# Decay factors of a gated DeltaNet layer: from matrix products of masked gates to differences of running sums spread by DMA

## The chip, the cores and the metric

The kernel runs on one NeuronCore of one Trainium2 chip. The core has a matrix engine (PE, with its weight loads shown apart as PEld), a vector engine (DVE), a scalar engine (ACT), a general engine (POOL) and a queue processor (SP) that issues most transfers. Each engine takes its instructions in the order in which they stand in its own list, and waits on semaphores of the others. The metric is the device time of one execution in microseconds. Before the change the median of three runs is 1008.61 us (1008.36 to 1009.39).

## The reference

Two layers act on 256 tokens of width 2048. Layer 0 is a gated DeltaNet with 16 heads of 128, layer 1 a banded softmax attention; each is `h = h + Mixer(RMSNorm(h))`. What matters here is how layer 0 gets its decays:

```python
g = -jnp.exp(a_log) * jax.nn.softplus(a_in + dt_bias)      # per token and head
gc = jnp.cumsum(g, axis=-1)
diff = gc[..., :, None] - gc[..., None, :]
decay = jnp.exp(jnp.where(tri_incl, diff, -jnp.inf))       # exp(gc_i - gc_j), lower triangle
lower = jnp.where(tri_strict, (k_beta @ k^T) * decay, 0.0)
qk = (q @ k^T) * decay
```

All weights and activations are float32. The kernel works on two token halves of 128 instead of chunks of 64, so for every head it needs three 128x128 blocks of factors `exp(gc_i - gc_j)`: the first half with itself, the second half against the first, the second half with itself.

## The kernel before, in words

The weights (168 MB) pass through the core once. A weight tile is 512 KB. It arrives in one of four `wt` buffers by a transfer that SP issues (L208), ACT rounds it to the matrix engine's reduced float format (`whi`, the cast at L209), DVE forms what the rounding left (`wlo = wt - whi`, L210), and PE multiplies both with the activations (L259). `whi` and `wlo` have three buffers each, and `LOOK = 3`: in the program's text the cast of tile i+3 stands ahead of the products of tile i, and it can start only when PE has read tile i's `whi` for the last time.

In the part of the program that is changed, the tiles hold 256 columns (the "half" kind). Such a tile takes eight products of 512 columns with `whi` and eight of 256 columns with `wlo`. With even numbers the `whi` products come first, with odd numbers the `wlo` products. Tiles are numbered here in the order of the plan, from 0: tiles 0 to 7 are the first query block, 8 to 15, 16 to 23 and 24 to 31 are the other three query blocks, 32 to 63 the key blocks.

Everything else is side work, written as Python generators in two lanes, `bgq` and `bg2`. After every four products of a half tile the helper `tick` runs a step: it takes turns between the lanes and lets one generator go on to its next `yield`. In the query stage `bgq` holds the short convolutions (`q_conv`, L527 and L529), SiLU and the transposes of the queries (`q_rest`, L546, L552, squares at L558), and `bg2` holds `decays()`, which makes the factors. The built order of each engine is then set by the framework's scheduler, which goes by its own estimate of times and by these positions; it doesn't change at run time.

`decays()` first computes the gates `g` for 128 tokens x 32 (16 heads, two halves). Until the change it goes on as follows, for four groups of four heads:

- DVE masks: `rhs(gi)` multiplies the lower-triangle mask `lt_f` with the gate of each head, once for the rounded gate `g_r` and once for its rest `gl_r` (L486, four 128x512 instructions a group).
- PE sums: six products of 512 columns a group, with the constant matrices `gt_r` and `ones_r` (L501), into three PSUM tiles. The result is already `gc_i - gc_j`.
- ACT exponentials: two 128x512 instructions (L506, L507) and four of 128x128 with a per-partition bias (L509), out of PSUM into `dec`, which lies in the buffer `dl`.
- DVE masks the two diagonal blocks (L516, two 128x512 instructions a group).

`dec` is used much later, in the key stage (L605), where it multiplies the key and query products. The buffer `tt`, which holds `rhs`'s results, is used again there.

Of the kernel before, what the change touches and what calls it, by code (L numbers as in the profile page):

```python
# [7 lines left out]
F32 = mybir.dt.float32  # L8
F32R = mybir.dt.float32r
# [30 lines left out]
def tile_hybrid_trunk(  # L40
# [22 lines left out]
    def ps_small():  # L63
        return pss.tile([P, 512], F32, name="pss", tag="pss")
# [5 lines left out]
    def slot(tag, kb, dt=F32):  # L70

        return big.tile([P, kb * 256], dt, name=tag, tag=tag)
# [12 lines left out]
    for _ in range(NWARM):  # L85
# [11 lines left out]
    gt_f = abm[:, 1024 + P:1024 + 2 * P]  # L97
    pool.memset(gt_f, 1.0)
    pool.affine_select(out=gt_f, in_=gt_f, compare_op=ALU.is_gt, fill=0.0, base=0,
                       pattern=[[-1, P]], channel_multiplier=1)  # L100
# [4 lines left out]
    gt_r = const.tile([P, P], F32R, name="gt_r")  # L105
    ones_r = const.tile([P, P], F32R, name="ones_r")
# [301 lines left out]
    def ht(name, dt=F32):  # L408
        return const.tile([P, H, 2], dt, name=name)

    beta, g_r, gl_r = ht("beta"), ht("g_r", F32R), ht("gl_r", F32R)
# [8 lines left out]
    def decays():  # L420
        act.copy(out=gt_r, in_=gt_f)
        act.copy(out=ones_r, in_=ones_f)

# [51 lines left out]
        dve.tensor_copy(out=g_r, in_=q)  # L475
        dve.tensor_tensor(out=gl_r, in0=q, in1=g_r.bitcast(F32), op=ALU.subtract)
        yield 1
        dve.tensor_scalar(out=eb, in0=eb, scalar1=1.0, scalar2=None, op0=ALU.add)
        dve.reciprocal(out=beta, in_=eb)

        rbuf = slot("tt", 16, F32R).rearrange("p (b k c) -> p b k c", b=2, k=4)

        def rhs(gi):
            for half in range(2):
                for part, src in ((0, g_r), (1, gl_r)):
                    dve.tensor_tensor(  # L486
                        out=rbuf[:, gi % 2, 2 * half + part, :].rearrange("p (h c) -> p h c", h=4),
                        in0=lt_f.unsqueeze(1).broadcast_to([P, 4, P]),
                        in1=src[:, 4 * gi:4 * gi + 4, half].bitcast(F32).unsqueeze(2).broadcast_to([P, 4, P]),
                        op=ALU.mult)  # L490

        rhs(0)
        yield 1
        rhs(1)
        yield 1
        for gi in range(4):
            hs = slice(4 * gi, 4 * gi + 4)
            ps3 = [ps_small() for _ in range(3)]
            for dst, lhs, half in ((ps3[0], gt_r, 0), (ps3[1], ones_r, 1), (ps3[2], gt_r, 1)):
                for part in range(2):  # L500
                    pe.matmul(dst, lhsT=lhs, rhs=rbuf[:, gi % 2, 2 * half + part, :],  # L501
                              start=(part == 0), stop=(part == 1))
            v0 = ps3[0].rearrange("p (h c) -> p h c", h=4)
            tail = tiny.tile([P, 4], F32, name="tail", tag="tail")
            dve.tensor_copy(out=tail, in_=v0[:, :, P - 1])
            act.activation(out=dec[:, hs, 0:128], in_=v0, func=AF.Exp)  # L506
            act.activation(out=dec[:, hs, 256:384], in_=ps3[2].rearrange("p (h c) -> p h c", h=4), func=AF.Exp)  # L507
            for i in range(4):
                act.activation(out=dec[:, 4 * gi + i, 128:256], in_=ps3[1][:, i * P:(i + 1) * P], func=AF.Exp,  # L509
                               bias=tail[:, i:i + 1])  # L510
            yield 1
            if gi < 2:
                rhs(gi + 2)
            yield 1
            for c in (0, 256):
                dve.tensor_tensor(out=dec[:, hs, c:c + 128], in0=dec[:, hs, c:c + 128],  # L516
                                  in1=lt_f.unsqueeze(1).broadcast_to([P, 4, P]), op=ALU.mult)
            yield 1
# [730 lines left out]
```

## Time and profile before

| | |
|---|---|
| median of three runs | 1008.61 us |
| the profiled execution | 1010.83 us, its span 1009.1 us |
| PE busy | 1001.4 us (99%), 6090 matmul records |
| DVE busy | 690.0 us (68%) |
| ACT busy | 526.6 us (52%) |
| POOL busy | 62.4 us (6%) |
| DMA | 177.57 MB, mean 176 GB/s |
| group L486 (masked gates), DVE | 16 instructions, 5.2 + 5.1 us |
| group L501 (sums), PE | 24 instructions, 5.3 + 2.6 us |
| groups L506, L507, L509 (exponentials), ACT | 24 instructions, 2.4 + 2.4 + 4.5 us |
| group L516 (masks), DVE | 8 instructions, 5.3 us |

A row of a group gives line, engine, operation, the tiles that it writes and reads, the shape, the count, then the busy time in us and the mean duration of one in ns, and behind a second bar the idle time of the engine ahead of it and what ended that. A row of the timeline gives start and duration in us, then engine, line, operation and count of one run of equal instructions. Since instructions of an engine overlap a little, the distance from one start to the next is what an instruction costs its engine, and is less than its duration. The first L501 starts at 82.4 us, the last at 103.7 us. The granted clock (PEclk) is the share of TensorE's full clock that the chip allows.

### The profile page before, as it was taken

To read this page: it belongs to the slowest core of one execution; us is meant where nothing else is said; L and a number is where in the kernel's file an instruction comes from. 1 tells how busy PE (TensorE), PEld (TensorE's weight loads), DVE (VectorE), ACT (ScalarE), POOL (GpSimd) and SP (SyncE) were. 2 spreads that over 40 slices of the span, in tenths; PEclk is the share of its full clock that TensorE was granted. 3 is DMA by queue.
4 is the path that set the end of the run, shared out by engine and by line. 5 is a ranking of instruction groups with operands and counts; after the bars stand their busy time and mean duration, and the time that the engine had idled before them with its cause. 6 is when DMAs were issued, how large, how long until landed. Compare 5 with 4: busy or idle time off the path is not lost.

```text
span 1009.1 us, 15660 instructions
## 1 busy us (share of the span) xinstructions
PE 1001.4 (99%) x6090; PEld 878.8 (87%) x6090; DVE 690.0 (68%) x1121; ACT 526.6 (52%) x784; POOL 62.4 (6%) x83
## 2 busy tenths in 40 slices
PE   8999999999999999999999999999999999999998
PEld 7988888888888899899988888888888888889987
DVE  5789979997998767755867555444456666666554
ACT  6557865565446555534645444444445555555432
POOL 1000001022000000001000000000011010101000
PEclk8999999999999999999999999999999999999999
DMA  8665565555665454535765776666665565554472
GB/s 285 169 169 167 158 185 145 160 160 167 197 186 163 131 148 145 167 127 180 237 188 183 224 219 204 193 191 194 199 186 169 148 178 155 167 157 157 158 230 92
DMA packets 134186, 177.57 MB, mean 176 GB/s; under 512 B 7904, under 2 KB 90208, under 8 KB 134112
## 3 DMA queue, kind: packets, MB, share of 16 engines
q1 hardware_dynamic: 132672, 172.12, 57.5%
q0 software_dynamic: 1152, 4.19, 1.2%
q8 instruction: 47, 0.77, 0.3%
q10 hardware_dynamic: 288, 0.26, 0.1%
q14 instruction: 27, 0.22, 0.1%
HBM read 174.46 MB, written 2.10 MB: 175 GB/s over the span
## 4 chain that ended last, share of the span: by engine, by line
PE 98%; DMA 1%; DVE 0%; ACT 0%; issue 0%; SPq 0%
PE psp L259 87%; PE pss L601 2%; PE pss L259 1%; PE pss L1068 1%; DMA wt<-in_a_w_in_dram 1%; PE pss L1087 1%; PE pss L1123 1%; PE pss L833 1%; PE pss L501 1%; PE pss L1113 1%; PE pss L857 0%; PE pss L856 0%; PE pss L840 0%; PE pss L858 0%; PE pss L1086 0%; PE pss L1124 0%
## 5 line engine op out<-in xcount | busy, mean ns | idle before, releaser
L210 DVE TENSOR_TENSOR wlo<-wt,whi 128x1024 fp32r<-128x1024 f32 (+1 forms) x322 | 391.2, 1218 | 244.9 <-ACT whi L209 241.0
L209 ACT CAST whi<-wt 128x1024 fp32r<-128x1024 f32 (+1 forms) x322 | 336.7, 1046 | 381.3 <-PE psp L259 331.8
L259 PE MATMUL psp<-whi,xb 128*128 128x512 f32 x1024 | 318.9, 391 | 0.0
L259 PE MATMUL psp<-xb,whi 128*128 128x512 f32 (+1 forms) x1088 | 261.4, 382 | 2.2 <-ACT whi L209 1.9
L259 PEld LDWEIGHTS psp<-xb,whi 128*128 128x128 f32 x1088 | 197.0, 191 | 36.4 <-ACT whi L209 2.5
L259 PEld LDWEIGHTS psp<-whi,xb 128*128 128x128 f32 x1024 | 191.7, 188 | 39.1
L259 PE MATMUL psp<-wlo,xb 128*128 128x512 f32 x512 | 200.8, 392 | 0.0
L259 PE MATMUL psp<-xb,wlo 128*128 128x256 f32 x1024 | 149.0, 285 | 0.7 <-DVE wlo L210 0.7
L259 PE MATMUL psp<-g,whi 128*128 128x256 f32 (+1 forms) x736 | 149.6, 318 | 0.0
L259 PEld LDWEIGHTS psp<-xb,wlo 128*128 128x128 f32 x1024 | 138.0, 192 | 6.6 <-DVE wlo L210 1.2
L259 PEld LDWEIGHTS psp<-g,whi 128*128 128x128 f32 x736 | 121.7, 191 | 8.4 <-DVE g L900 0.2
L259 PEld LDWEIGHTS psp<-wlo,xb 128*128 128x128 f32 x512 | 96.2, 188 | 19.7
L259 PE MATMUL psp<-g,wlo 128*128 128x256 f32 x480 | 101.9, 284 | 0.3 <-DVE wlo L210 0.3
L259 PEld LDWEIGHTS psp<-g,wlo 128*128 128x128 f32 x480 | 77.8, 191 | 1.7 <-DVE wlo L210 0.5
L529 DVE SCALAR_TENSOR_TENSOR cv<-raw,sm,cv 128x255 f32<-128x255 f32 (+2 forms) x144 | 63.8, 477 | 3.4 <-ACT cv L527 3.2
L527 ACT ACTIVATE cv<-raw,sm 128x256 f32<-128x256 f32 x48 | 22.5, 509 | 20.6 <-DVE raw L345 20.6
L1051 POOL TENSOR_SCALAR ssn<-ssn,uh 128x4 f32<-128x4 f32 x16 | 8.3, 530 | 266.8 <-DVE ssn L1049 266.8
L330 DVE TENSOR_TENSOR ev<-psp,ev 128x512 f32<-128x512 f32 x33 | 22.6, 684 | 0.1
L329 ACT COPY ev<-psp 128x512 f32<-128x512 f32 x33 | 19.1, 579 | 0.0
L1099 ACT ACTIVATE raw<-raw,mx 128x128 f32<-128x128 f32 (+1 forms) x32 | 14.2, 446 | 7.4 <-DVE mx L1097 7.4
L605 DVE TENSOR_TENSOR dl<-pss,dl 128x512 f32<-128x512 f32 (+1 forms) x32 | 16.3, 551 | 2.7 <-PE pss L601 2.7
L1058 DVE TENSOR_TENSOR cv<-psp,rn 128x512 f32<-128x512 f32 x16 | 10.2, 683 | 8.9 <-POOL rn L1053 8.9
(233 smaller groups left out, 742.4 us busy)
## 6 DMA issues: line engine op xcount, KB each, us to landing
wt<-in_b_w_in_dram SPq DMA_DIRECT2D x128, 512.0 KB, 3.7
wt<-in_a_w_in_dram SPq DMA_DIRECT2D x127, 512.0 KB, 4.0
wt<-in_a_w_out_dram SPq DMA_DIRECT2D x32, 512.0 KB, 3.8
wt<-in_b_w_out_dram SPq DMA_DIRECT2D x32, 512.0 KB, 3.9
dl<-in_xT_dram POOLq DMA_DIRECT2D x4, 512.0 KB, 5.8
dl<-in_relb_dram POOLq DMA_DIRECT2D x4, 512.0 KB, 4.9
g<-in_xT_dram SPq DMA_DIRECT2D x7, 256.0 KB, 5.2
out_dram<-cv SPq DMA_DIRECT2D x2, 512.0 KB, 3.5
```

The costliest lines, as they stand in the source:

```text
L209: cast = act.copy(out=hi[:, js, cs], in_=wt[:, js, cs])
L210: rest = dve.tensor_tensor(out=lo[:, js, cs], in0=wt[:, js, cs], in1=hi[:, js, cs].bitcast(F32), op=ALU.subtract)
L259: state["mm"] = pe.matmul(*args, **kw).ins
L329: act.copy(out=ev, in_=ps[:, :, 1, :])
L330: dve.tensor_tensor(out=ev, in0=ps[:, :, 0, :], in1=ev, op=ALU.add)
L501: pe.matmul(dst, lhsT=lhs, rhs=rbuf[:, gi % 2, 2 * half + part, :], start=(part == 0), stop=(part == 1))
L527: act.activation(out=cv[:, i, :], in_=raw[:, i, :], func=AF.Copy, scale=conv_w(i0 + i, 3))
L529: dve.scalar_tensor_tensor(out=cv[:, i, s:], in0=raw[:, i, :T - s], scalar=conv_w(i0 + i, 3 - s), in1=cv[:, i, s:], op0=ALU.mult, op1=ALU.add)
L601: pe.matmul(dst, lhsT=kq[:, a, i, c:c + P], rhs=rhs, start=(n == 0), stop=(n == 2))
L605: dve.tensor_tensor(out=dl[:, h, :, c], in0=src.rearrange("p (k c) -> p k c", k=2), in1=dec[:, h, c].unsqueeze(1).broadcast_to([P, 2, n]), ...
L1058: dve.tensor_tensor(out=n[:, t, :].rearrange("p (h d) -> p h d", d=P), in0=ps[:, t, :].rearrange("p (h d) -> p h d", d=P), in1=rn[:, t, :] ...
L1099: act.activation(out=s[:, a:b], in_=s[:, a:b], func=AF.Exp, bias=mx[:, t:t + 1], accum_out=sums[:, t:t + 1])
```

## The change

The constants `gt_f`, `gt_r` and `ones_r`, the rounded gates and `rhs` go. Two small float32 products with `lt_f` give the running sums of the gates, once with heads on the partitions (32x128) and once with tokens on the partitions (128x32). The first goes by DMA to a DRAM tile `line` and from there, in four transfers of 512 KB, to all 128 partitions of `tt`: every partition then has the running sums of all heads along its row. The second, with its sign changed, is `ngc`. Nine `yield`s follow. Then, for each group of four heads, POOL copies the two diagonal blocks from `tt` to `dec` and writes -1e30 outside the triangle (`affine_select`), and adds the bias `across` for the third block; after a `yield`, ACT takes the exponentials of one head to a `yield`, three 128x128 instructions with a per-partition bias, from SBUF.

```diff
@@ def decays():
-        act.copy(out=gt_r, in_=gt_f)
-        act.copy(out=ones_r, in_=ones_f)
...
-        dve.tensor_copy(out=g_r, in_=q)
-        dve.tensor_tensor(out=gl_r, in0=q, in1=g_r.bitcast(F32), op=ALU.subtract)
-        yield 1
+        gf = q.rearrange("p h t -> p (h t)")
         dve.tensor_scalar(out=eb, in0=eb, scalar1=1.0, scalar2=None, op0=ALU.add)
         dve.reciprocal(out=beta, in_=eb)
...
-        rhs(0)
-        yield 1
-        rhs(1)
-        yield 1
+        yield 1
+        ps = ps_small()
+        pe.matmul(ps[0:32, 0:P], lhsT=gf, rhs=lt_f, start=True, stop=True)
+        pe.matmul(ps[:, P:P + 32], lhsT=lt_f, rhs=gf, start=True, stop=True)
+        grow = abm[0:32, 1280:1280 + P]
+        dve.tensor_copy(out=grow, in_=ps[0:32, 0:P])
+        ngc = const.tile([P, H, 2], F32, name="ngc")
+        dve.tensor_scalar(out=ngc, in0=ps[:, P:P + 32].rearrange("p (h t) -> p h t", t=2), scalar1=-1.0, scalar2=None,
+                          op0=ALU.mult)
+        line = rows.tile([32, P], F32, name="line")
+        nc.gpsimd.dma_start(out=line, in_=grow)
+        gb = slot("tt", 16).rearrange("p (j c) -> p j c", c=P)
+        for gi in range(4):
+            js = slice(8 * gi, 8 * gi + 8)
+            nc.gpsimd.dma_start(out=gb[:, js, :], in_=line[js, :].unsqueeze(0).broadcast_to([P, 8, P]))
+        for _ in range(9):
+            yield 1
+        gb = gb.rearrange("p (h t) c -> p h t c", t=2)
+        across = const.tile([P, H], F32, name="across")
         for gi in range(4):
             hs = slice(4 * gi, 4 * gi + 4)
-            ps3 = [ps_small() for _ in range(3)]
-            for dst, lhs, half in ((ps3[0], gt_r, 0), (ps3[1], ones_r, 1), (ps3[2], gt_r, 1)):
-                for part in range(2):
-                    pe.matmul(dst, lhsT=lhs, rhs=rbuf[:, gi % 2, 2 * half + part, :],
-                              start=(part == 0), stop=(part == 1))
...
-            act.activation(out=dec[:, hs, 0:128], in_=v0, func=AF.Exp)
-            act.activation(out=dec[:, hs, 256:384], in_=ps3[2].rearrange("p (h c) -> p h c", h=4), func=AF.Exp)
-            for i in range(4):
-                act.activation(out=dec[:, 4 * gi + i, 128:256], in_=ps3[1][:, i * P:(i + 1) * P], func=AF.Exp,
-                               bias=tail[:, i:i + 1])
...
-            for c in (0, 256):
-                dve.tensor_tensor(out=dec[:, hs, c:c + 128], in0=dec[:, hs, c:c + 128],
-                                  in1=lt_f.unsqueeze(1).broadcast_to([P, 4, P]), op=ALU.mult)
-            yield 1
+            for t in range(2):
+                pool.affine_select(out=dec[:, hs, 2 * P * t:2 * P * t + P], in_=gb[:, hs, t, :], compare_op=ALU.is_ge,
+                                   fill=NEG, base=0, pattern=[[0, 4], [1, P]], channel_multiplier=-1)
+            pool.tensor_tensor(out=across[:, hs], in0=gb[:, hs, 0, P - 1], in1=ngc[:, hs, 0], op=ALU.add)
+            yield 1
+            for h in range(4 * gi, 4 * gi + 4):
+                for c, src, b in ((0, dec[:, h, 0:P], ngc[:, h, 0:1]), (P, gb[:, h, 1, :], across[:, h:h + 1]),
+                                  (2 * P, dec[:, h, 2 * P:3 * P], ngc[:, h, 1:2])):
+                    act.activation(out=dec[:, h, c:c + P], in_=src, func=AF.Exp, bias=b)
+                yield 1
```

The scheduler moves instructions with it. In the changed kernel the lines behind the removed ones have smaller numbers: L203 is the cast of L209, L204 the rest of L210, L253 the products of L259, L509 the scaling of L527, L528 the SiLU of L546, L534 the transposes of L552, L540 the squares of L558; L499 are the new exponentials.

The first place is ACT, from the first exponentials on. `whi` is the rounded weight tile, `dl` holds `dec`, `sj` is the output of a square that nobody reads, and the tables are the sets of functions that ACT loads. Before, from the last cast ahead of them:

```order
L209 CAST whi<-wt 128x1024 x4
L329 COPY ev<-psp 128x512
L507 ACT_TABLE_LOAD
L507 ACTIVATE dl<-pss 128x4x128
L527 ACTIVATE cv<-raw,sm 128x256 x2
L209 CAST whi<-wt 128x1024
L506 ACTIVATE dl<-pss 128x4x128
L509 ACTIVATE dl<-pss,tail 128x128 x4
L209 CAST whi<-wt 128x1024
L506 ACTIVATE dl<-pss 128x4x128
L509 ACTIVATE dl<-pss,tail 128x128 x4
L209 CAST whi<-wt 128x1024
```

With the change, from the cast of tile 27 over that of tile 28:

```order
L203 CAST whi<-wt 128x1024
L540 ACTIVATE sj,ssq<-pss 128x128 x4
L499 ACT_TABLE_LOAD
L499 ACTIVATE dl<-dl,ngc 128x128 x4
L509 ACTIVATE cv<-raw,sm 128x256 x2
L499 ACTIVATE dl<-dl,ngc 128x128 x3
L499 ACTIVATE dl<-tt,across 128x128 x4
L499 ACTIVATE dl<-dl,ngc 128x128
L203 CAST whi<-wt 128x1024
L499 ACTIVATE dl<-dl,ngc 128x128 x4
L499 ACTIVATE dl<-tt,across 128x128 x2
```

The rows that follow are L499 alone, until the last one of the 48:

```order
L499 ACTIVATE dl<-tt,across 128x128
L499 ACTIVATE dl<-dl,ngc 128x128
L528 ACT_TABLE_LOAD
L528 ACTIVATE g<-cv 128x1024
L203 CAST whi<-wt 128x1024 x3
```

Before, no more than six exponential instructions stood between two casts. Now 12 of the 48 stand between the casts of tiles 27 and 28, and the other 36, a table load and a SiLU between the casts of tiles 28 and 29.

The second place is PE, from the second half of tile 22 on. `pss` are the small PSUM tiles, `psp` the accumulators of the weight products. Before:

```order
L259 MATMUL psp<-xb,wlo 128x256 x14
L501 MATMUL pss<-tt,gt_r 128x512
L259 MATMUL psp<-xb,wlo 128x256 x2
L501 MATMUL pss<-tt,ones_r 128x512
L501 MATMUL pss<-tt,gt_r 128x512
L259 MATMUL psp<-xb,whi 128x512 x2
```

With the change, up to the products of tile 29 (the ten `wlo` products are eight of tile 22 and two of tile 23, the row of eight transposes stands between tiles 28 and 29):

```order
L253 MATMUL psp<-xb,wlo 128x256 x10
L472 MATMUL pss<-kT 32x128
L473 MATMUL pss<-kT 128x32
L534 MATMUL pss<-ident,g 128x128 x12
L253 MATMUL psp<-xb,wlo 128x256 x6
L253 MATMUL psp<-xb,whi 128x512 x16
L534 MATMUL pss<-ident,g 128x128 x4
L253 MATMUL psp<-xb,wlo 128x256 x16
L253 MATMUL psp<-xb,whi 128x512 x16
L253 MATMUL psp<-xb,wlo 128x256 x16
L253 MATMUL psp<-xb,whi 128x512 x16
```

```order
L253 MATMUL psp<-xb,wlo 128x256 x8
L534 MATMUL pss<-ident,g 128x128 x8
L253 MATMUL psp<-xb,wlo 128x256 x8
L253 MATMUL psp<-xb,whi 128x512 x16
```

The 24 sums of L501 are gone, two short products stand in tile 23, and twelve transposes of the queries have moved ahead into tile 23 and four into tile 24.

More of the change, by code (lines that the diff above doesn't have):

```diff
@@ L96, in tile_hybrid_trunk @@
                        pattern=[[1, P]], channel_multiplier=-1)
[L97 to L100, printed above, removed]
     ones_f = const.tile([P, P], F32, name="ones_f")
@@ L104, in tile_hybrid_trunk @@
     pool.memset(nhalf, -0.5)
-    gt_r = const.tile([P, P], F32R, name="gt_r")
-    ones_r = const.tile([P, P], F32R, name="ones_r")
     def rsqrt(dst, src, scale, bias):
@@ L409, in ht @@
         return const.tile([P, H, 2], dt, name=name)
-    beta, g_r, gl_r = ht("beta"), ht("g_r", F32R), ht("gl_r", F32R)
+    beta = ht("beta")
+    rows = ctx.enter_context(tc.tile_pool(name="rows", bufs=1, space=bass.MemoryType.DRAM))
     dl = slot("dl", 48).rearrange("p (h k c) -> p h k c", h=H, k=2)
@@ L474, in decays @@
                                  op0=ALU.mult, op1=ALU.mult)
-        dve.tensor_copy(out=g_r, in_=q)
-        dve.tensor_tensor(out=gl_r, in0=q, in1=g_r.bitcast(F32), op=ALU.subtract)
-        yield 1
+        gf = q.rearrange("p h t -> p (h t)")
         dve.tensor_scalar(out=eb, in0=eb, scalar1=1.0, scalar2=None, op0=ALU.add)
         dve.reciprocal(out=beta, in_=eb)
[L481 to L490, printed above, removed]
@@ L496, in decays @@
         for gi in range(4):
             hs = slice(4 * gi, 4 * gi + 4)
-            ps3 = [ps_small() for _ in range(3)]
-            for dst, lhs, half in ((ps3[0], gt_r, 0), (ps3[1], ones_r, 1), (ps3[2], gt_r, 1)):
-                for part in range(2):
-                    pe.matmul(dst, lhsT=lhs, rhs=rbuf[:, gi % 2, 2 * half + part, :],
-                              start=(part == 0), stop=(part == 1))
-            v0 = ps3[0].rearrange("p (h c) -> p h c", h=4)
-            tail = tiny.tile([P, 4], F32, name="tail", tag="tail")
@@ L505, in decays @@
-            dve.tensor_copy(out=tail, in_=v0[:, :, P - 1])
-            act.activation(out=dec[:, hs, 0:128], in_=v0, func=AF.Exp)
-            act.activation(out=dec[:, hs, 256:384], in_=ps3[2].rearrange("p (h c) -> p h c", h=4), func=AF.Exp)
-            for i in range(4):
-                act.activation(out=dec[:, 4 * gi + i, 128:256], in_=ps3[1][:, i * P:(i + 1) * P], func=AF.Exp,
-                               bias=tail[:, i:i + 1])
-            yield 1
-            if gi < 2:
-                rhs(gi + 2)
```

## The prediction

> **What bounds the kernel now.** I read the page first: busy time, the slices, the chain that ended last.
>
> ```profile
> span 1009.1 us, 15660 instructions
> PE 1001.4 (99%) x6090; PEld 878.8 (87%) x6090; DVE 690.0 (68%) x1121; ACT 526.6 (52%) x784; POOL 62.4 (6%) x83
> PEclk8999999999999999999999999999999999999999
> PE 98%; DMA 1%; DVE 0%; ACT 0%; issue 0%; SPq 0%
> ```
>
> PE is the chain. A busy PE is not yet a PE at its peak, so I looked at the stretch of the change, in windows (PE, PEld, DVE, ACT, POOL, clock, DMA share, GB/s) and in the timeline of PE.
>
> ```profile
> 80.00:90.00 10.00, 10.00 (x61) 8.82 (x60) 10.00 (x16) 5.41 (x8) 0.00 (x0) 1.00 0.55 160
> 90.00:100.00 10.00, 10.00 (x54) 8.58 (x53) 10.00 (x19) 8.82 (x19) 0.00 (x0) 1.00 0.51 138
> 100.00:110.00 10.00, 10.00 (x59) 8.71 (x58) 10.00 (x19) 8.34 (x24) 0.00 (x0) 1.00 0.58 149
> ```
>
> ```profile
> 91.03 3.33 PE L259 MATMUL psp<-xb,whi 128*128 128x512 f32 x14
> 94.20 1.08 PE L501 MATMUL pss<-tt,gt_r 128*128 128x512 f32 x4
> 95.12 1.10 PE L259 MATMUL psp<-xb,wlo 128*128 128x256 f32 x8
> 96.06 1.77 PE L259 MATMUL psp<-xb,whi 128*128 128x512 f32 x7
> ```
>
> From start to start: 14 products in 3.17 us (0.226 each), four sums of L501 in 0.92 (0.23 each), eight `wlo` products in 0.94 (0.118 each). They follow each other without a hole. DVE is full in the same 30 us (10.00 of 10.00), yet PE never waits for it: taking work off DVE wins nothing here, taking work off PE does, one for one. A weight tile costs PE 8 x 0.226 + 8 x 0.118 = **2.75 us**.
>
> How far ahead of PE the tiles are made ready is in the waits of the whole run (total, times, longest).
>
> ```profile
> ACT whi L209 <- PE psp L259: 331.8, 214, 5.1
> DVE wlo L210 <- ACT whi L209: 241.0, 199, 4.3
> ```
>
> ACT's casts wait for PE to free one of three buffers, so the lead is what three buffers hold and no more. Whatever keeps ACT from a cast for longer than that lead stops PE, and PE has no slack anywhere later to win it back.
>
> **The change part by part.**
>
> *PE's work.* 24 sums go: 24 x 0.23 = -5.5 us. Two float32 products come. The nearest row is one that the program has four times and the trace eight, each in two passes:
>
> ```profile
> L387 PE MATMUL pss<-dg,ones_f 128*128 128x128 f32 x8 | 1.2, 274 | 0.0
> ```
>
> 1.2 / 8 = 0.15 a pass, four passes: +0.6. Net **-4.9 us**, all on the path. The moved transposes are the same number as before.
>
> *DVE's work.* Sixteen L486 and eight L516 at some 0.6 us go, two small copies come. Priced at nothing: PE's products covered them, as the windows show. If that cover were gone, wlo rather than these would be late.
>
> *ACT's work, where the stall goes.* 24 exponential instructions become 48, of 128 columns, from SBUF, with a bias per partition. The one row of that very form is in layer 1:
>
> ```profile
> 822.26 1.05 ACT L209 CAST whi<-wt 128x1024 fp32r<-128x1024 f32 x1 [2.98 <-PE psp L259]
> 823.21 0.39 ACT L1099 ACTIVATE raw<-raw,mx 128x128 f32<-128x128 f32 x1
> 823.51 0.19 ACT L1099 ACTIVATION_READ_ACCUMULATOR raw<-raw,mx 128x1 f32 x1
> 100.57 1.13 ACT L509 ACTIVATE dl<-pss,tail 128x128 f32<-128x128 f32 x4
> 111.29 1.28 ACT L546 ACT_TABLE_LOAD   x1
> 112.59 1.06 ACT L546 ACTIVATE g<-cv 128x1024 f32<-128x1024 f32 x1
> 113.55 0.26 ACT L558 ACTIVATE sj<-pss 128x128 f32<-128x128 f32 x1
> 113.71 0.19 ACT L558 ACTIVATION_READ_ACCUMULATOR sj<-pss 128x1 f32 x1
> 113.80 0.27 ACT L558 ACTIVATE sj<-pss 128x128 f32<-128x128 f32 x1
> L210 DVE TENSOR_TENSOR wlo<-wt,whi 128x1024 fp32r<-128x1024 f32 x319 | 389.6, 1224 | 244.3 <-ACT whi L209 240.3 <-PE psp L259 3.3
> L527 ACT ACTIVATE cv<-raw,sm 128x256 f32<-128x256 f32 x48 | 22.5, 509 | 20.6 <-DVE raw L345 20.6
> ```
>
> The exponential of L1099 holds ACT for 823.51 - 823.21 = 0.30 us; L509, out of PSUM, for about 0.25 (four in 1.13, the last one 0.37 long). A whole duration without overlap would be 0.39. I take 0.30, the same operands; ends 0.25 and 0.39. A cast costs ACT 0.95, a SiLU 0.96, a square with its read 0.25, an L527 about 0.4 to 0.5.
>
> The yields ask for three exponentials a step, but ACT follows the built order, where they stand together. I start both clocks at the end of the four transposes in the middle of tile 24, which the squares behind the cast of tile 27 wait for.
>
> ACT from there to the point where tile 29 can start: four squares 1.0, table 1.28, 48 exponentials 14.4, two L527 0.9, cast of tile 28 0.95, table 1.28, SiLU 0.96, cast of tile 29 1.05, and then DVE's rest of tile 29 1.22 (an odd tile begins with `wlo`). Sum **23.0 us**.
>
> PE from there to tile 29: eight `wlo` products 0.9, tiles 25 to 28 4 x 2.75 = 11.0, eight transposes 0.8. Sum **12.7 us**.
>
> So PE stands still for **+10.3 us** ahead of tile 29. Behind the waiting cast are the casts of tiles 30 and 31 and SP's next weight transfer; PE waits for all of them, and they come at 1 us each once ACT is free, faster than PE needs them. The eight transposes wait for the SiLU behind the exponentials and then fit under the cast. The nine yields themselves cost nothing: the factors are first read behind tile 46 of the built order, 17 tiles or 47 us after tile 29.
>
> *The data of the first exponential.* The sums come by two transfers in a row through POOL's queue.
>
> ```profile
> 80.77 1.84 PE L259 MATMUL psp<-xb,wlo 128*128 128x256 f32 x14
> 82.44 0.39 PE L501 MATMUL pss<-tt,gt_r 128*128 128x512 f32 x1
> dl<-in_relb_dram POOLq DMA_DIRECT2D x4, 512.0 KB, 4.9
> dl<-in_xT_dram POOLq DMA_DIRECT2D x4, 512.0 KB, 5.8
> sm<-in_small_dram SPq DMA_DIRECT2D x1, 16.0 KB, 2.2
> L95 POOL TENSOR_SCALAR_AFFINE_SELECT kT<-kT x1: 287/287/287, 1.8 to 1.8; 128x128 f32<-128x128 f32 x1
> L651 POOL MEMSET tt<- 128x4096 f32 x1 | 3.5, 3535 | 17.1 <-PE pss L601 17.1
> ```
>
> On the clock of this trace the eighth of the fourteen `wlo` products ends at about 81.7 and tile 23 begins. DVE copies the sums out behind the rest of tile 25 (1.22, not before 81.7) and one L345: about 83.9. The 16 KB line lands 2.2 to 4.9 us later, the first 512 KB 4.9 to 5.8 after that, a select of 512 columns takes about 0.6 (0.29 for 128, and 3535 / 4096 = 0.86 ns for each further column): data at 91.6 to 95.2. ACT gets there at 81.7 + 0.9 (`wlo`) + 0.6 + 1.3 (twelve transposes) + 16 x 0.226 + 0.4 (four transposes) = 88.5, and 2.3 on for squares and table: 90.8. Late by 0.8 to 4.4; I take **+1.5**, near the lower end, since the line is small. The later three quarters land while ACT works 3.6 us a quarter: 512 KB in 3.6 us is 146 GB/s beside the 138 to 160 of the windows, below the 345 seen here:
>
> ```profile
> 8.00:10.00 2.00, 1.28 (x10) 1.07 (x10) 0.68 (x2) 0.91 (x2) 0.00 (x0) 1.00 0.96 322
> 10.00:12.00 2.00, 0.78 (x2) 0.50 (x2) 1.00 (x2) 1.81 (x3) 0.27 (x1) 0.69 1.06 393
> 12.00:15.00 3.00, 2.54 (x13) 2.52 (x12) 2.55 (x5) 2.55 (x7) 0.49 (x2) 0.50 1.01 345
> 15.00:20.00 5.00, 5.00 (x34) 5.00 (x34) 4.42 (x9) 3.89 (x8) 0.81 (x2) 0.74 1.04 344
> ```
>
> *The clock.* The same rows price what a stall does to PE: after PE had been partly idle from 8 to 12 us, its granted clock was 0.69, 0.50 and 0.74, that is halved for 1.2 + 3.0 + 2.6 = 6.8 us. A stall of 10 us is longer than that one was. Halved for up to 6.8 us of work costs at most 3.4 us; part of it falls into the stall itself. I take **+2.4**, ends 0 and 3.4.
>
> The Trainium skill, page "TensorE: Matmul & The Clock Gate", section "Part 1: The HAM clock gate", has the clock at half after an idle window of about 3.4 us and at full again after one busy window. By that rule the loss would be 1.7 to 3.4 us, and the sum 1017.2 to 1018.9. The 6.8 us here agree with two such windows.
>
> **Sum**, for the profiled execution of 1010.83 us (span 1009.1, 1.7 around it): -4.9 + 10.3 + 1.5 + 2.4 = +9.3, so 1020.1. The median of the runs is 2.2 below that execution: 1008.6 + 9.3 = 1017.9, **1018 us**.
>
> **The rivals.**
>
> *The exponentials hide, faster.* If PE found tile 29 ready, the 24 sums would be won: 1008.6 - 4.9 = **1003.7**. For it speaks that every wait of PE in this stretch is zero today, with up to six exponential instructions between casts. Against it: ACT's 23.0 us would have to fall to 12.7, that is 48 exponentials in 4 us, 0.08 each, where the shortest row of that width is a square out of PSUM at 0.16 (113.55 to 113.71). At that price the stall is 3.6, hardly long enough for the clock, and the data's lateness then makes it about 1008: no change. Both together 11 in 100.
>
> *The spread data starve ACT.* 128 partitions read the same 4 KB, a pattern that no row has, and POOL's selects may be held up:
>
> ```profile
> L625 POOL TENSOR_SCALAR ssk<-ssk x4: 241/778/1161, 173.2 to 247.3; 128x8 f32<-128x8 f32 x4
> L628 POOL TENSOR_TENSOR rk<-rk,beta 128x8 f32<-128x8 f32 x4 | 2.6, 653 | 0.3
> ```
>
> The same operation takes 0.24 or 1.16. With 0.92 more on two selects and one addition a quarter needs 2 x 0.6 + 0.65 + 2.8 = 4.6 us on POOL, 1 us over ACT's 3.6, three times: +3; first data at their late end: +2.9. That is **1024**; with a slow repeated read, more. Against it: DVE, whatever its part, is idle itself while PE stalls. 12 in 100. The Trainium skill ("GPSIMD Engine Reference", "Key points") says that POOL shares its SBUF ports with DVE and is held up by DVE instructions with two SBUF inputs; by that rule the result would be this one, and no row here shows which instruction held L625 up.
>
> *The stall without the clock*, 1015.5, lies inside the forecast's range.
>
> **How the numbers follow.** The forecast of a stall of 8 to 15 us has 77 in 100, starving 12, no change 5, faster 6. Low end: exponentials at 0.25 (-2.4), data at their early end (-0.7), no clock loss (-2.4): 1012.5. High end: exponentials at 0.39 alone would give +4.3, clock +1.0, and the starving case 1024 and up. Range 1012 to 1025. Within 0.2% (2 us, about what a measurement of this kernel tells from no change): 5 in 100, faster 6, slower 89.
>
> **What would show it.** Right: in the changed profile a hole in PE's row of 9 to 13 us at about 100 to 113 us, ended by ACT (the SiLU of L528, then `wlo` of L204), ACT full from 91 to 113 with 48 L499 at 0.30 each, the granted clock at 0.5 behind the hole, no L501, and the rest of the run as before, shifted. Wrong: no hole (then the first rival), a hole already ahead of tile 28 with ACT idle on POOL or a DMA (the second), or L499 under 0.2 us apart.

## The result and the profile after

| | before | after |
|---|---|---|
| median | 1008.57 us (4 runs, 1008.36 to 1009.39) | 1018.51 us (4 runs, 1016.86 to 1018.71) |
| the profiled execution, its span | 1010.83, 1009.1 us | 1018.71, 1017.0 us |

The change makes the kernel 9.9 us slower: ratio 1.0094, 95% interval 1.0081 to 1.0107. From the page of the changed kernel: span, busy time, the slices of PE and of its clock, and the chain that ended last.

```profile
span 1017.0 us, 15646 instructions
PE 997.7 (98%) x6070; PEld 874.7 (86%) x6070; DVE 677.8 (67%) x1093; ACT 531.2 (52%) x806; POOL 72.0 (7%) x98
PE   8998699999999999999999999999999999999998
PEclk9999799999999999999999999999999999999999
PE 94%; ACT 3%; DVE 1%; issue 1%; DMA 1%; SPq 0%; POOL 0%; DVEq 0%; POOLq 0%
```

PE is busy for less time than before (997.7 against 1001.4) and yet ends later. One slice, the fifth (102 to 127 us), has lost a third of PE and a quarter of its clock, and ACT has entered the chain with 3%, about 30 us. The windows of that stretch (PE, PEld, DVE, ACT, POOL, clock, DMA share, GB/s):

```profile
90.00:100.00 10.00, 8.30 (x48) 6.98 (x47) 4.90 (x7) 8.09 (x25) 6.88 (x11) 1.00 0.73 260
100.00:110.00 10.00, 0.38 (x4) 0.18 (x2) 0.00 (x0) 9.97 (x29) 0.39 (x2) 0.66 0.19 54
110.00:115.00 5.00, 4.55 (x18) 4.06 (x19) 3.87 (x4) 5.00 (x18) 0.00 (x0) 0.50 0.22 60
115.00:120.00 5.00, 5.00 (x23) 4.10 (x23) 1.46 (x2) 2.25 (x7) 0.00 (x0) 0.81 0.77 257
```

From 100 to 110 us PE does 0.38 us of work, ACT 9.97. The weight transfers stop too (54 GB/s): all four `wt` buffers are full, and SP waits 12.9 us until a `wlo` frees one. The timeline of the same kernel shows who waits for whom (start, duration, and in brackets the idle time ahead and what ended it).

```profile
78.15 1.35 PE L253 MATMUL psp<-xb,wlo 128*128 128x256 f32 x10
91.23 1.23 POOL L492 TENSOR_SCALAR_AFFINE_SELECT dl<-tt 128x512 f32<-128x512 f32 x2 [2.98 <-DMA tt<-line]
91.91 1.28 ACT L499 ACTIVATE dl<-dl,ngc 128x128 f32<-128x128 f32 x4 [2.53 <-POOL dl L492]
96.24 1.03 ACT L203 CAST whi<-wt 128x1024 fp32r<-128x1024 f32 x1
97.32 2.11 PE L253 MATMUL psp<-xb,whi 128*128 128x512 f32 x8 [1.70 <-ACT whi L203]
99.27 1.12 PE L253 MATMUL psp<-xb,wlo 128*128 128x256 f32 x8
107.41 0.39 ACT L499 ACTIVATE dl<-dl,ngc 128x128 f32<-128x128 f32 x1
109.11 1.06 ACT L528 ACTIVATE g<-cv 128x1024 f32<-128x1024 f32 x1
110.07 2.92 ACT L203 CAST whi<-wt 128x1024 fp32r<-128x1024 f32 x3
110.22 1.97 PE L534 MATMUL pss<-ident,g 128*128 128x128 f32 x8 [9.84 <-ACT g L528]
111.14 3.50 DVE L204 TENSOR_TENSOR wlo<-wt,whi 128x1024 fp32r<-128x1024 f32 x3 [12.14 <-ACT whi L203]
112.42 2.07 PE L253 MATMUL psp<-xb,wlo 128*128 128x256 f32 x8 [0.23 <-DVE wlo L204]
114.29 5.04 PE L253 MATMUL psp<-xb,whi 128*128 128x512 f32 x16
```

From the list of transfers (size, then median us from issue to landing):

```profile
line<-kT POOLq DMA_DIRECT2D x1, 16.0 KB, 3.8
```

The first exponential waits for POOL, and POOL for the DMA. The cast of tile 28 stands behind 12 exponentials and is late by 1.70 us. Then 36 exponentials, the table and the SiLU stand ahead of the cast of tile 29. PE is done with tile 28 at 100.39 and waits 9.84 us for the SiLU. Afterwards everything on PE is slow: eight transposes 1.97 us, eight `wlo` products 2.07, sixteen `whi` products 5.04. The same runs of instructions at full clock take 1.04, 1.11 and 3.82 (rows of two other runs below). That is 0.93 + 0.96 + 1.22 = 3.1 us.

So: 1.70 + 9.84 + 0.23 + 3.1 = 14.9 us lost, and 4.9 us of PE's work less by the prediction's term: +10.0. The medians differ by 9.94, but the interval of the ratio allows 8.2 to 10.8 us, so the close agreement is luck.

The ends of products are modelled, and a wait looks shorter by them. Counted from one start to the next, the loss is 15.5 us and the sum +10.6. The two profiles say the same: from the first `wlo` of tile 22 (78.15 us here, 80.77 before) to the end of the span the changed kernel takes 938.8 us where it took 928.3, 10.5 more. So nothing that is lost in this stretch is won back behind it.

### The profile page after: what moved, and what is told of

It is laid out like the page before. It is cut to its first block, busy times and chain, and to the rows that moved or that the text cites. A ratio compares the mean times of both kernels' runs of the same rounds, so it can differ in the third digit from the quotient of the medians.

```text
span 1017.0 us, 15646 instructions
## 1 busy us (share of the span) xinstructions
PE 997.7 (98%) x6070; PEld 874.7 (86%) x6070; DVE 677.8 (67%) x1093; ACT 531.2 (52%) x806; POOL 72.0 (7%) x98
## 4 chain that ended last, share of the span: by engine, by line
PE 94%; ACT 3%; DVE 1%; issue 1%; DMA 1%; SPq 0%; POOL 0%; DVEq 0%; POOLq 0%
PE psp L253 83%; PE pss L583 2%; ACT dl L499 1%; PE pss L253 1%; PE pss L1050 1%; PE pss L1069 1%; PE pss L1105 1%; PE pss L815 1%; DMA wt<-in_a_w_in_dram 1%; DVE wlo L204 1%; PE pss L1095 1%; ACT whi L203 1%; PE pss L839 0%; PE pss L838 0%; PE pss L822 0%
## 5 line engine op out<-in xcount | busy, mean ns | idle before, releaser
L204 DVE TENSOR_TENSOR wlo<-wt,whi 128x1024 fp32r<-128x1024 f32 (+1 forms) x322 | 391.6, 1219 | 261.0 <-ACT whi L203 256.7
L203 ACT CAST whi<-wt 128x1024 fp32r<-128x1024 f32 (+1 forms) x322 | 335.9, 1045 | 382.9 <-PE psp L253 333.2
L253 PE MATMUL psp<-whi,xb 128*128 128x512 f32 x1024 | 318.8, 391 | 0.0
L253 PE MATMUL psp<-xb,whi 128*128 128x512 f32 (+1 forms) x1088 | 259.3, 381 | 3.3 <-ACT whi L203 2.7
L253 PEld LDWEIGHTS psp<-xb,whi 128*128 128x128 f32 x1088 | 196.0, 190 | 38.2 <-ACT whi L203 3.3
L253 PEld LDWEIGHTS psp<-whi,xb 128*128 128x128 f32 x1024 | 191.7, 188 | 39.0
L253 PE MATMUL psp<-wlo,xb 128*128 128x512 f32 x512 | 200.8, 392 | 0.0
L253 PE MATMUL psp<-g,whi 128*128 128x256 f32 (+1 forms) x736 | 149.6, 318 | 0.1
L253 PE MATMUL psp<-xb,wlo 128*128 128x256 f32 x1024 | 148.3, 285 | 1.2 <-DVE wlo L204 1.2
L253 PEld LDWEIGHTS psp<-xb,wlo 128*128 128x128 f32 x1024 | 137.3, 192 | 7.2 <-DVE wlo L204 2.0
L253 PEld LDWEIGHTS psp<-g,whi 128*128 128x128 f32 x736 | 121.7, 190 | 8.4 <-DVE g L882 0.3
L253 PEld LDWEIGHTS psp<-wlo,xb 128*128 128x128 f32 x512 | 96.1, 188 | 19.7
L253 PE MATMUL psp<-g,wlo 128*128 128x256 f32 x480 | 101.9, 284 | 0.3 <-DVE wlo L204 0.3
L253 PEld LDWEIGHTS psp<-g,wlo 128*128 128x128 f32 x480 | 77.7, 191 | 1.7 <-DVE wlo L204 0.5
L509 ACT ACTIVATE cv<-raw,sm 128x256 f32<-128x256 f32 x48 | 22.5, 505 | 21.0 <-DVE raw L339 21.0
L851 POOL TENSOR_TENSOR ro<-so,nhalf 128x8 f32<-128x8 f32 x4 | 6.5, 1636 | 156.0 <-DVE so L849 156.0
```

The lines of the kernel that those rows point to most:

```text
L203: cast = act.copy(out=hi[:, js, cs], in_=wt[:, js, cs])
L204: rest = dve.tensor_tensor(out=lo[:, js, cs], in0=wt[:, js, cs], in1=hi[:, js, cs].bitcast(F32), op=ALU.subtract)
L253: state["mm"] = pe.matmul(*args, **kw).ins
L509: act.activation(out=cv[:, i, :], in_=raw[:, i, :], func=AF.Copy, scale=conv_w(i0 + i, 3))
```

## The experiments

**The kernel before once more.** The profiled execution of before was 2.2 us above the median. Nothing is edited; this asks where these 2.2 us lay.

> The kernel before once more, for a second profile of it. In the first profile PE lost 6.35 us to waits and a halved clock in its first 20 us, in the profile of the change 2.75, though nothing differs there. Theory (the start varies from run to run, so the two profiles differ by less than the medians do): the same holes later, the loss of the start anywhere between 2.7 and 6.4 us, the time about 1008.6 or up to 1011 with it. Rival (the change shortens the start by 3.6 us): the loss stays at 6.3 us in every profile of the kernel before.

Windows (columns as above) of 10 to 20 us and of the stretch of the change, in the second profile:

```profile
10.00:20.00 10.00, 9.21 (x73) 8.91 (x73) 9.13 (x15) 8.94 (x19) 1.30 (x4) 1.00 1.05 365
80.00:110.00 30.00, 30.00 (x174) 26.27 (x173) 30.00 (x50) 23.54 (x56) 0.00 (x0) 1.00 0.50 142
```

1008.5 us. The clock stays at 1.00 at the start, where the first profile had 0.69, 0.50 and 0.74; PE lost 2.9 us there instead of 6.35 (what its instructions take from start to start, over the usual distance of their kind). The start varies from run to run and is no part of the change; the first `wlo` of tile 22, at 80.77 us in the first profile, comes at 78.44 in the second, and these 2.3 us are the whole difference of the two spans (PE's first weight product stands 0.8 us earlier in the first profile, at 5.19 in place of 6.00, which makes up for a part of its loss). In the stretch of the change PE is full in both profiles.

**More empty steps: 32, and 22.** The only edit is the number of empty steps ahead of the exponentials, here for 32; the other run has 22 in the same place. With 0, 4 or 14 of them the exponentials stand in the same portions between the casts as with nine, 12 and 36; with 22 they are 12, 21, 3, 6 and 6, with 32 they are 9, 8, 7, 3, 8, 2, 8 and 3.

```diff
-        for _ in range(9):
+        for _ in range(32):
             yield 1
```

> The changed kernel with 32 empty steps ahead of the exponentials instead of nine; nothing else differs. In the built order the 48 exponentials then stand in eight portions of 2 to 9 between the casts of nine tiles, instead of 36 between two casts. Theory (the place of the exponentials on ACT makes the stall): no hole over 3 us, the clock stays full, 1018.5 - 10.7 (hole) - 2.7 (cold clock) - 1.9 (late data) = 1003.2, plus up to 5 us where a portion of 7 to 9 exponentials or the table load and the SiLU still makes a cast late: 1004 to 1009. Rival (the spread rows or the exponentials out of SBUF cost by themselves, wherever they stand): 1014 or more. Rival (the first exponential waits for the DMA and that is the whole delay): 1016, only the 1.9 us of late data go.

> The changed kernel with 22 empty steps instead of nine. In the built order 21 exponentials stand between the casts of tiles 28 and 29 instead of 36, the rest in portions of 3 and 6 behind. Theory (the number of exponentials ahead of that cast sets the hole): 36 - 21 = 15 exponentials of 0.29 us less, 10.7 - 4.4 = 6.3 us of hole, a clock that still halves as it did behind the hole of 6.8 us with narrow exponentials (1.4 us there), later stalls of 1 to 2 us: 1018.5 - 4.4 - 1.4 = 1012.7, plus or minus 1.5. Rival (any portion longer than the lead costs the same): 1017 or more. Rival (half of the portions already fit): 1009, as with 32 steps.

| exponentials ahead of the cast of tile 29 | wait of PE for it or the SiLU | median | ratio to before |
|---|---|---|---|
| 36 (the change) | 9.84 + 0.23 us | 1018.51 us | 1.0094 (1.0081 to 1.0107) |
| 21 (22 steps) | 5.27 us | 1013.24 us | 1.0042 (1.0026 to 1.0057) |
| 8 (32 steps) | 1.70 us | 1009.06 us | 1.0009 (1.0001 to 1.0018) |

With 22 steps, in the timeline:

```profile
106.35 2.07 PE L253 MATMUL psp<-xb,wlo 128*128 128x256 f32 x8 [5.27 <-DVE wlo L204]
```

With 32 steps, in the timeline:

```profile
91.89 1.28 ACT L499 ACTIVATE dl<-dl,ngc 128x128 f32<-128x128 f32 x4 [2.25 <-POOL dl L492]
96.43 2.11 PE L253 MATMUL psp<-xb,whi 128*128 128x512 f32 x8 [0.55 <-ACT whi L203]
99.71 1.58 DVE L204 TENSOR_TENSOR wlo<-wt,whi 128x1024 fp32r<-128x1024 f32 x1 [1.32 <-ACT whi L203]
101.34 1.22 PE L253 MATMUL psp<-xb,wlo 128*128 128x256 f32 x8 [1.70 <-DVE wlo L204]
104.25 1.04 PE L534 MATMUL pss<-ident,g 128*128 128x128 f32 x8
106.50 2.11 PE L253 MATMUL psp<-xb,whi 128*128 128x512 f32 x8 [1.22 <-ACT whi L203]
108.45 1.11 PE L253 MATMUL psp<-xb,wlo 128*128 128x256 f32 x8
110.08 1.22 PE L253 MATMUL psp<-xb,wlo 128*128 128x256 f32 x8 [0.52 <-DVE wlo L204]
```

The portion ahead of one cast sets the wait: 15 exponentials fewer shorten it by 4.6 us (15 x 0.29 = 4.4 were expected; the time, 1013.24 us, lies in the expected 1012.7 plus or minus 1.5). The table load and the SiLU have moved behind the cast with 22 steps, but that changes the wait little: they take 2.4 us in the change, where the wait ends with the SiLU, and the cast and the `wlo`, with which it ends here, take 2.3. With 32 steps the data come at 91.89 us, as in the change (91.91), so they are not the hole. With 32 steps the exponentials begin as early as in the change, from the same buffers, at the same pace, and cost almost nothing net; the rival that they cost by themselves falls. But the result lies at the end of the expected range, not at 1003: four waits of 0.55, 1.70, 1.22 and 0.52 us remain, together 4.0 (5.4 counted from start to start), each from a cast behind 3 to 9 exponentials, one of them behind a SiLU and two table loads as well; in the wait of 1.70 the `wlo` itself is also slow, 1.58 us where 1.22 is usual. They eat what PE's work won. The clock stays full in this stretch.

**Narrow exponentials.** Order, number, transfers and selects as in the change; only the width of the 48 instructions is cut (two memsets on POOL, ahead and behind, put zeros in place of the factors).

```diff
-                    act.activation(out=dec[:, h, c:c + P], in_=src, func=AF.Exp, bias=b)
+                    act.activation(out=dec[:, h, c:c + 8], in_=src[:, 0:8], func=AF.Exp, bias=b)
```

> The changed kernel with every exponential cut to its first 8 columns of 128 (the factors are left out by this: they are zero). The order on ACT is the same, 36 exponentials between two casts, and so are their number, the DMAs and the selects. Theory (ACT's time for the exponentials is the length of the hole): an exponential costs about 0.19 instead of 0.29 us, the hole gets 36 x 0.10 = 3.6 us shorter, about 7; the clock is still halved behind it: 1014 to 1016. Rival (the hole hangs on the DMA, the selects or the waits between them): 1018, hole of 10 us. If the instruction costs the same 0.29 us at any width, theory and rival are not told apart and the pace of the group will say so.

Rows of the timeline and of the windows:

```profile
99.34 0.48 ACT L500 ACTIVATE dl<-dl,ngc 128x8 f32<-128x8 f32 x2
99.91 0.48 ACT L500 ACTIVATE dl<-dl,ngc 128x8 f32<-128x8 f32 x2
105.49 1.97 PE L536 MATMUL pss<-ident,g 128*128 128x128 f32 x8 [6.62 <-ACT g L530]
```

```profile
100.00:110.00 10.00, 4.29 (x19) 3.80 (x20) 3.60 (x4) 9.97 (x34) 5.22 (x1) 0.66 0.16 43
```

1013.02 us, ratio 1.0047 (1.0033 to 1.0061). An exponential of 8 columns costs ACT 0.19 us (99.91 - 99.34 = 0.57 for three), so 36 of them are 3.6 us shorter and the 12 ahead of them 1.2; PE comes to the hole 1.5 us sooner; 3.6 + 1.2 - 1.5 = 3.3, and the wait falls by 3.2, from 9.84 to 6.62. The rest of the gain is the cast of tile 28, which now stands behind 12 shorter ones and is hardly waited for (0.2 us), and the clock, which is at half for 6.8 us (0.34 x 10 x 2) instead of 13.7. The expected 1014 to 1016 had left out the 12 exponentials ahead of tile 28. The hole follows ACT's time for the exponentials; DMA and selects were untouched.

**PE kept busy through the hole.** This run is meant to tell the clock's share from the stall's. The built order moves a little with it: all 48 exponentials stand ahead of the cast of tile 28 here, and the added products come earlier than the hole did, amid the `whi` products of tile 25.

```diff
         yield 1
+        if gi == 2:
+            ps = ps_small()
+            for _ in range(48):
+                pe.matmul(ps, lhsT=xb[:, 0, 0, 0:P], rhs=xb[:, 0, :, :], start=True, stop=True)
         for p in range(2):
```

> The changed kernel with 48 products of 512 columns added on PE, whose results nobody reads, ahead of the transposes of this stretch: 48 x 0.227 = 10.9 us, about as long as the hole, so that PE works through it. All 48 exponentials then stand between two casts. Theory (the halved clock costs 2.7 us behind the hole): PE has no gap over 1.5 us, the clock stays at 1.00, 1018.5 - 2.7 = 1015.8 (1015 to 1017). Rival (the clock shown costs nothing, the products after the hole are slow for another reason): 1018.5 and products of 0.43 us behind it. Rival (the added products do not fall into the hole): 1018.5 + 10.9 = 1029.

```profile
90.18 11.05 PE L533 MATMUL pss<-xb 128*128 128x512 f32 x48
108.85 2.14 PE L253 MATMUL psp<-xb,whi 128*128 128x512 f32 x8 [1.15 <-ACT whi L203]
```

```profile
100.00:110.00 10.00, 8.85 (x47) 7.32 (x46) 1.17 (x1) 9.98 (x29) 0.00 (x0) 1.00 0.00 0
```

1017.5 us (1017.2 to 1019.96), ratio 1.0096 (1.0081 to 1.0112). 11 us of added work on PE cost nothing: the hole was free time, as the theory says, and ACT is the bound there. The clock stays at 1.00, as expected. But the time did not fall by the expected 2.7 us; by the medians it fell by 1.0, and the intervals overlap. In the profiled execution 10.9 us of added work and 2.5 us of waits stand in place of waits and slow products of 15.5 us (both counted from start to start). That is 2.1 us less, and 1.1 us of it is lost again at the start of the run, where the clock fell this time. So the slow products are real, 3.1 us by their rows, but what a warm clock gives back in all is between nothing and some 2 us by these runs. The trace of the change shows why it can't be all of the 3.1: the 0.93 us of the transposes would not have been won, since PE waited another 0.23 us behind them for tile 29's `wlo`, which DVE had only at 112.4 us (111.14 and 1.23 for one). That leaves 2.2 us, close to the 2.1 of the profiled executions.

**PE's work, one for one.** In the kernel before, the products with the rest of the gates are left out.

```diff
-                for part in range(2):
-                    pe.matmul(dst, lhsT=lhs, rhs=rbuf[:, gi % 2, 2 * half + part, :],
-                              start=(part == 0), stop=(part == 1))
+                pe.matmul(dst, lhsT=lhs, rhs=rbuf[:, gi % 2, 2 * half, :], start=True, stop=True)
```

> The kernel before with 12 of its 24 sum products left out (those with the rest of the rounded gates, so that the factors lack their lower bits); nothing else differs. Theory (PE's work in this stretch counts one for one, as the first term of the sum had it): 12 x 0.23 = 2.75 us less, 1005.8 (1005.3 to 1006.5). Rival (something else, a cast, the DMA or DVE's masks, is close behind PE): 1007 to 1008.5.

1006.32 us against 1008.84, ratio 0.9972 (0.996 to 0.9983): 2.5 us less, between 1.7 and 4.0, for 12 products. The first term of the prediction holds: by these 12, 24 products are worth about 5 us when nothing comes in their place.

**A version for which ACT has less to do.** DVE adds the bias for four heads at once, POOL masks in place, and ACT takes 12 exponentials of 512 columns. The lines below take the place of the selects and the 48 exponentials; 26 stands for 26, 32, 34 or 36 empty steps.

```diff
-        for _ in range(9):
+        for _ in range(26):
...
+            for c, t, b in ((0, 0, ngc[:, hs, 0]), (P, 1, across[:, hs]), (2 * P, 1, ngc[:, hs, 1])):
+                if c == P:
+                    pool.tensor_tensor(out=across[:, hs], in0=gb[:, hs, 0, P - 1], in1=ngc[:, hs, 0], op=ALU.add)
+                dve.tensor_tensor(out=dec[:, hs, c:c + P], in0=gb[:, hs, t, :],
+                                  in1=b.unsqueeze(2).broadcast_to([P, 4, P]), op=ALU.add)
+                if c != P:
+                    pool.affine_select(out=dec[:, hs, c:c + P], in_=dec[:, hs, c:c + P], compare_op=ALU.is_ge,
+                                       fill=NEG, base=0, pattern=[[0, 4], [1, P]], channel_multiplier=-1)
+                yield 1
+            for c in (0, P, 2 * P):
+                act.activation(out=dec[:, hs, c:c + P], in_=dec[:, hs, c:c + P], func=AF.Exp)
+                yield 1
```

> The spread rows stay, but DVE adds the bias of four heads at once (12 additions of 512 columns), POOL masks the two diagonal blocks in place, and ACT takes 12 exponentials of 512 columns instead of 48 of 128, after 26 empty steps. Theory (what the change costs is ACT's time in one place; what it wins is PE's sums, 4 us): 12 x 0.55 = 6.6 us of ACT in place of 48 x 0.29 = 13.9, spread between casts, stalls of 0 to 2 us: 1008.5 - 4.0 + 0 to 2 = 1004.5 to 1006.5, faster than the kernel before. Rival (12 additions of 0.65 us, 7.8 us on DVE, make wlo late, or POOL masks in place too slowly): 1008 or more, with holes ended by DVE.

> The same as the run with 26 empty steps, with 32. Theory: the same 1004.5 to 1006.5, since both spread the exponentials over several tiles; a difference of over 1 us would say that single portions still stop PE and which.

With 26 steps 1010.68 us, ratio 1.0016 (1.0007 to 1.0025); with 32 steps 1007.95, ratio 0.999 (0.9981 to 0.9999). Both miss the expected 1004.5 to 1006.5, the first by far. The timeline with 26 steps:

```profile
96.05 0.63 ACT L501 ACTIVATE dl<-dl 128x512 f32<-128x512 f32 x1 [3.47 <-POOL dl L497]
97.63 1.03 ACT L203 CAST whi<-wt 128x1024 fp32r<-128x1024 f32 x1
98.42 1.65 DVE L204 TENSOR_TENSOR wlo<-wt,whi 128x1024 fp32r<-128x1024 f32 x1
100.12 2.08 PE L253 MATMUL psp<-xb,wlo 128*128 128x256 f32 x8 [2.55 <-DVE wlo L204]
```

An exponential for four heads is now 0.63 us long, where four of 0.29 stood. But ACT stands idle for 3.47 us ahead of the first, waiting for POOL's mask, with the cast behind it: the rival that the prediction had at 12 in 100, data that starve ACT, shows up once ACT itself is cheap. And the hole of 2.55 us halves the clock again.

One attempt put all additions and masks first and the exponentials later (23 empty steps ahead and 12 between, or 26 and 16):

```diff
+        for _ in range(12):
+            yield 1
+        for gi in range(4):
+            hs = slice(4 * gi, 4 * gi + 4)
             for c in (0, P, 2 * P):
```

> The version with 12 wide exponentials, but with the additions and masks of all four groups ahead (after 23 empty steps), 12 more empty steps, and only then the exponentials, so that on ACT no exponential stands ahead of a cast before its masked data are there. Theory (the hole of 2.8 us in the two wide versions came from a cast behind exponentials that waited for POOL's masks, and the halved clock of 1.4 us from that hole): at most one stall of 1.6 us, clock full, 1008.6 - 4.0 + 0.5 to 2.5 = 1005 to 1007. Rival (DVE and POOL slow one another: 1.65 us for a wlo of 1.22, so the work itself is too much for the stretch): 1008 or more, with holes ended by DVE.

> The same with 26 and 16 empty steps. Theory: the exponentials come later still, no stall at 95 to 110 us, but the key stage follows sooner upon them; 1004.5 to 1008, and where it is above the other version the loss stands behind 400 us.

1011.64 us, ratio 1.0027 (1.0016 to 1.0039), and 1016.21, ratio 1.0074 (1.006 to 1.0087): worse. In the first of them the cast is in time, and DVE is what is late:

```profile
94.32 1.73 DVE L494 TENSOR_TENSOR dl<-tt,ngc 128x512 f32<-128x512 f32 x2
95.61 1.05 ACT L203 CAST whi<-wt 128x1024 fp32r<-128x1024 f32 x1 [2.70 <-PE psp L253]
97.01 2.01 DVE L517 SCALAR_TENSOR_TENSOR cv<-raw,sm,cv 128x255 f32<-128x255 f32 x3
98.94 1.21 DVE L204 TENSOR_TENSOR wlo<-wt,whi 128x1024 fp32r<-128x1024 f32 x1
100.21 1.22 PE L253 MATMUL psp<-xb,wlo 128*128 128x256 f32 x8 [2.82 <-DVE wlo L204]
```

The cast ends at 96.66, and `wlo` starts 2.3 us later, behind additions and convolutions on DVE. Two of the additions run beside POOL's selects and take 1.12 and 1.11 us, where 0.68 is usual. A second wait of 2.59 us for a `wlo` follows. The rival holds here, not the theory. The second version has two such waits as well (2.91 and 2.60 us), where none was expected, and another 5 us go behind 400 us (waits of 1.02, 0.95, 0.73 and 0.83 us ahead of PE at 443 to 479 us). The likely reason is that the later steps push the other side work into the key stage; no run isolates it.

Last, the wide exponentials in the first arrangement, two and four steps later than with 32:

> The version with 12 wide exponentials after 34 empty steps instead of 32. In the run with 32 one hole of 2.8 us was left: the cast of tile 28 stood behind two exponentials that waited for POOL's masks of the spread rows. Theory (that one hole and the halved clock behind it, 4.2 us together, are all that is left, and another built order around them moves the exponentials off the late data): 1004 to 1007. Rival (the lateness of data, DVE and POOL beside each other leaves a hole of 2 to 3 us in any order of this kind): 1008 to 1011.

> The same with 36 empty steps, where one exponential fewer stands ahead of the cast of tile 28. Theory: 1004 to 1007. Rival: 1008 to 1011. The two together tell whether the rest depends on the single place in the order.

1006.67 us, ratio **0.9978** (0.9969 to 0.9987), and 1006.84, ratio 0.9984 (0.9975 to 0.9993). Both lie in the expected 1004 to 1007, at its upper end. With 34 steps one wait of over 0.2 us is left in this stretch, ahead of the same tile:

```profile
97.46 1.40 ACT L501 ACTIVATE dl<-dl 128x512 f32<-128x512 f32 x2 [3.98 <-POOL dl L497]
101.11 1.22 PE L253 MATMUL psp<-xb,wlo 128*128 128x256 f32 x8 [1.69 <-DVE wlo L204]
102.17 3.82 PE L253 MATMUL psp<-xb,whi 128*128 128x512 f32 x16
```

It is 1.69 us, and the clock stays full behind it (sixteen `whi` products in 3.82 us). This is a version with the spread running sums that is faster than both kernels, by 2 us against before. It is the best of six versions of this kind, but the intervals of both runs, 34 and 36 steps, exclude the time of before. Of the 5 us of PE's work about 2 are kept.

## Why the prediction held, step by step

It said 1018.0 and a stall; 1018.51 was measured.

- *PE's work, -4.9.* Held: 12 products were worth 2.5 us (1.7 to 4.0) against 2.75 expected, and the two float32 products cost 0.58 us (79.43 to 80.01) where 0.6 was taken. The profiles of before and after say 5.0 for the whole term: 15.5 us lost on PE, 10.5 us more time.
- *DVE's work, nothing.* No run isolates it. DVE does nothing for the whole hole (0.00 from 100 to 110 us), so taking work off it won nothing here; where additions were put on it, in the wide versions, `wlo` was what came late.
- *The stall, +10.3, and the data's lateness, +1.5.* The mechanism held: ACT full, the exponentials at 0.29 (four in 1.28 us, the last 0.39 long; 0.30 was taken), and three runs with 21, 8 or narrow exponentials moved the wait as ACT's time does. What ended the wait was the SiLU for the transposes, as the observable named, and the `wlo` of tile 29 was then late by 0.23 only. The sum held as well, 1.70 + 9.84 + 0.23 = 11.8 us, but the split didn't, and that is luck. ACT stood idle for 2.53 us ahead of the first exponential, not 1.5, which leaves 9.2 us for the stall. It is shorter than 10.3 mainly because the eight transposes ran inside it at half clock and kept PE at work for 1.97 us, where 0.8 was taken.
- *Why the data came later.* The profile of the change runs 2.6 us ahead of the one that the prediction used (78.15 against 80.77), so its 92.3 for the first exponential is 89.7 there; it started at 91.91. The mis-sized item is the small transfer: the 16 KB line took 3.8 us to land, where its size had spoken for the lower end of 2.2 to 4.9. ACT itself was ready 1.2 us later than predicted (89.4 in place of 88.2), which hid a part.
- *The hole ahead of tile 28.* The prediction put the whole delay ahead of tile 29. A hole already ahead of tile 28, with ACT idle on POOL or a DMA, was its sign of being wrong, and this sign is there: 1.70 us. It is the second rival in small, far from the 1024 us that it was given, and behind the first exponential ACT waits for no data any more. That the wait is a matter of the 12 exponentials ahead of the cast as much as of the data shows in the narrow version: the first exponential started only 0.3 us sooner (91.62), and of the wait 0.2 us was left.
- *The clock, +2.4.* The slow products cost 3.1 us by their rows, inside 0 to 3.4, and 2.2 of it lie where a full clock could have won time. The clock was halved for 13.7 us, not 6.8; 7.0 us of that fell into the hole and 6.7 on PE's work, so the price came out near the bound all the same.
- *The nine yields, nothing.* Held, and more: by the built order up to 14 of them move no exponential past a cast.
- *The rivals.* "The exponentials hide" fell: it needs a place in the order that nine steps don't reach, and even 32 steps only brought the time to that of before. Its step that a stall of 3.6 us is hardly long enough for the clock fell too, since a hole of 2.55 us halved it. "Starving ACT" took 1.70 us here and decided in the versions with wide exponentials, through POOL's masks.

None of this hangs on the start of the run: by tile 22 the two first profiles differ by 2.6 us, and the 10.5 us are counted from there.

## What to carry to other kernels

An engine that is half idle over the span can still be the bound of a stretch: count what stands on it between two instructions that the chain waits for, and compare with what the chain's engine has to do in that time. A `yield` or any lead in the program's text moves nothing by itself; read the built order to see whether the portions between such instructions changed. Where side work is made cheaper on one engine, ask at once which engine feeds it, since here DMA, POOL and DVE were the next in line within 3 us.

## What was not expected of the hardware

- The clock falls and rises in steps of about 3.4 us. Halved time, worked out from the windows: 6.8 us around the hole of 6.62 (0.34 x 10 x 2), 13.7 around that of 9.84 ((0.34 x 10 + 0.5 x 5 + 0.19 x 5) x 2), two and four times 3.4. Around the hole of 2.65 in the wide version with 32 steps it was 3.4 (0.17 x 10 x 2). After the long hole PE had been at work for 6.7 us before the clock was full again (110.22 to about 116.9). The Trainium skill, page "TensorE: Matmul & The Clock Gate", section "Part 1: The HAM clock gate", has full clock after one busy window of about 3.4 us. That agrees with the size of the steps here; behind the long hole PE needed about two of them.
- In the stretch of the change holes of 1.69 and 1.70 us left the clock full, one of 2.55 us halved it:

```profile
104.77 4.69 PE L253 MATMUL psp<-xb,whi 128*128 128x512 f32 x16
```

  (26 steps and wide exponentials, against 3.82 for the same sixteen products. That is no safe size for every hole: at the start of the run with the added products, two waits of 1.23 and 0.76 us one after the other (at 10.54 and 11.80 us) were followed by a halved clock, and a wait of 1.08 us at the start of the run with 32 steps was not.)
- DVE and POOL hold one another up, and in these rows the one that starts second waits. In the changed kernel:

```profile
96.45 1.47 POOL L492 TENSOR_SCALAR_AFFINE_SELECT dl<-tt 128x512 f32<-128x512 f32 x2
97.30 1.69 DVE L204 TENSOR_TENSOR wlo<-wt,whi 128x1024 fp32r<-128x1024 f32 x1 [0.47 <-ACT whi L203]
97.89 1.16 POOL L494 TENSOR_TENSOR across<-tt,ngc 128x4 f32<-128x4 f32 x1
100.19 0.19 POOL L494 TENSOR_TENSOR across<-tt,ngc 128x4 f32<-128x4 f32 x1
```

  The `wlo` starts while a select has 0.62 us left to run (to 97.92) and takes 1.69 us, where 1.22 is usual; with 32 steps one starts with 0.51 us of a select left and takes 1.58. The small addition starts beside the running `wlo` and ends together with it (98.99 and 99.05): 1.16 us, where it takes 0.19 alone. It doesn't slow the `wlo` in turn: POOL's instructions overlap 29 of these in the changed kernel, and 27 of them take 1.21 to 1.24 us. The other slow one (1.47 us, at 310.64) also starts beside a running instruction of POOL, a copy. The Trainium skill, page "GPSIMD Engine Reference", section "Key points", names such DVE instructions with two SBUF inputs as those that contend with POOL. The rows agree, and add that DVE loses time as well.
